# Exchanging the scratch slots of two temporaries in the mixing layers of a fused two-block network

## The chip, the cores and the metric

The kernel runs on one core of a Trainium2 chip. The metric is the device time of one execution in microseconds (us), the median of several runs. The kernel before takes 1500.32 us (three runs, 1500.16 to 1500.45).

## The reference

One call computes two blocks over a sequence of 256 tokens with 1024 features, all in float32. The first block has two attention layers (a convolution beside one attention, then two kinds of sparse attention). The second block, run after it, has two layers of this form:

```
x = x + 0.5 * swiglu(rms_norm(x, ffn1_norm[l]), ...)
h = rms_norm(x, mix_norm[l])
proj = h @ w_in[l]
y_rwkv = rwkv7_group(proj[..., :RWKV_IN], ...)     # a recurrence over time, 8 heads of 64
y_ret = retnet_group(proj[..., RWKV_IN:])          # retention, 4 heads
x = x + concat(y_rwkv, y_ret) @ w_out[l]
x = x + 0.5 * swiglu(rms_norm(x, ffn2_norm[l]), ...)
```

The recurrence updates a 64x64 state per head: S <- S*diag(w) + (S a) b^T + v k^T, y = S r. Its output is normalised per head and gated. Retention rotates q and k, masks the scores q k^T by a decay, multiplies them with v and normalises per head.

## The kernel before, in words

Features lie on the 128 partitions, the 256 tokens along the free axis. Every weight is streamed from memory once, in parts of 128x1024, through a ring: SyncE issues the load into `raw` (4 slots, line 108), ScalarE casts it to `whi` (line 115), VectorE forms the rest `wlo` (line 116); `whi` and `wlo` have 5 slots each. A projection of 256 output features takes two such parts and 48 matmuls of 256 columns (three products per weight tile: lines 129 to 131, or 306 to 308 where tokens become the output rows). Its result stands in one of two PSUM banks of the tag `mm` until VectorE or ScalarE has read it.

A mixing layer (`mix`) works on the eight heads in two units of four. Unit 0 projects k, r and v, prepares the operands (`operands`), and builds its chunk matrices (`chunks`): gram matrices (line 980), then five levels of a triangular inverse, each level a `t1` and a `dx` (line 963) on TensorE with a mask, an addition and a transpose on VectorE between them (lines 1022, 1028, 1029). Unit 1 does the same. Then `chain` runs the recurrence of both units side by side, four chunks each, and ends with the last step: mean, squares, head sums (line 900), the reciprocal root in small VectorE steps (lines 172 to 180), the head norm factors widened by ScalarE (`wide`, line 887), transposed by TensorE (`spread`, line 891), and the gate (line 1105). After that comes `retention`: the projections rq and rk (read out into `rx`, line 1149, then rotated, lines 1155 to 1160), rv in two halves, rg in two halves, then scores (line 1189, masked into `rsc`), values and norms, and the output projection.

Scratch tiles come from a pool in which a tag names a ring of slots; here `pd` and `pz` have two slots each. A new tile of a tag takes the slot of the tile two before it and may be written only when that one's readers are done, in the order in which the program asks for the tiles. In the kernel before, `pz` holds the projection read out of PSUM in `shifted` (line 852) and later the masked scores; `pd` holds the token-shifted product (line 855), `wide`, `rx` and `rgt` (the read-out gate projection of retention).

The order of the instructions on an engine is not the program's order. A list scheduler places each instruction on its engine's queue when, by its own estimate, operands and slots are free; on the chip each queue then runs in that fixed order. So a change of slots changes the order.

Of the kernel before, what the change touches and what calls it, by code (L numbers as in the profile page):

```python
# [9 lines left out]
F32 = mybir.dt.float32  # L10
# [41 lines left out]
class Net:  # L52
# [771 lines left out]
    def mix(self, tag, l, cst):  # L824
# [6 lines left out]
        with ExitStack() as c:  # L831
            psum = self.banks.using(mm=(0, 1), ch=(2, 4), ss=(3,), inv=(5, 6), y=(7, 3))
            work = c.enter_context(tc.tile_pool(name="mw", bufs=1))
# [49 lines left out]

            def spread2(rn, tag):

                wide = work.tile([128, 2, 4, 64], F32, tag="pd", name="wide", bufs=2)
                nc.scalar.copy(wide, rn[:, :, :, None].to_broadcast([128, 2, 4, 64]))
                ps = psum.tile([128, 2, S], F32, tag=tag, name="spread")
                for u in range(2):
                    for tt in range(2):  # L890
                        nc.tensor.transpose(ps[:, u, tt * 128:tt * 128 + 128],
                                            wide[:, tt, 2 * u:2 * u + 2].rearrange("p e d -> p (e d)"), ident)
                return ps
# [19 lines left out]
            def operands(q, b):  # L913
# [24 lines left out]
                for u in range(2):  # L938
                    nc.vector.scalar_tensor_tensor(kq[:, u], r[:, u], self.v(f"rk{l}", 2 * b + u), kh[:, u],
                                                   op0=OP.mult, op1=OP.mult)  # L940
                yield
                sp = spread2(rn, "inv")
                nc.vector.tensor_tensor(kk, kk, sp, op=OP.mult)
                ps = psum.tile([128, 2, S], F32, tag="inv", name="bonus")
# [90 lines left out]
            def chain(q, b):  # L1035
# [58 lines left out]
                rn = self.rsqrt(by_head(y2, "ch"), [128, 2, 4], 1.0 / 64, 64e-5, "q")  # L1094
                yield
                sp = spread2(rn, "ch")
                nc.vector.tensor_tensor(y, y, sp, op=OP.mult)
                for u in range(2):
# [42 lines left out]
    def retention(self, tag, l, psum, work, cst, units):  # L1141
        nc = self.nc
        qk = {}
        qs = {}

        def project(name):
            ps = self.proj_t(psum, (tag, name))
            q = qs[name] = work.tile([128, 2, S], F32, tag="pd", name="rx", bufs=2)
            nc.vector.tensor_tensor(q, ps, self.rsb, op=OP.mult)

        def rotate(name):
            q = qs[name]
            ps = psum.tile([128, 2, S], F32, tag="mm", name="rot")
            for u in range(2):
                nc.tensor.matmul(ps[:, u], cst["rot"], q[:, u], start=True, stop=True)
            b = lambda m: m[:, None, :].to_broadcast([128, 2, S])
            o = qk[name] = work.tile([128, 2, S], F32, tag={"rq": "pr", "rk": "pk"}[name], name=name)
            nc.vector.tensor_tensor(o, ps, b(cst["sin"]), op=OP.mult)
            nc.vector.tensor_tensor(q, q, b(cst["cos"]), op=OP.mult)
            nc.vector.tensor_tensor(o, o, q, op=OP.add)  # L1160

        project("rq")
        project("rk")
        rotate("rq")
        v = work.tile([128, 2, 512], F32, tag="op1", name="rv")
        for b in range(2):
            ps = self.proj_n(psum, (tag, "rv", b))
            if b == 0:
                rotate("rk")
            for tt in range(2):  # L1170
                nc.scalar.activation(v[:, tt, 256 * b:256 * b + 256], ps[:, tt], AF.Copy,
                                     scale=self.rstok[:, tt:tt + 1])
        g = work.tile([128, 4, S], F32, tag="op2", name="rg")
        for b in range(2):
            ps = self.proj_t(psum, (tag, "rg", b))
            t = work.tile([128, 2, S], F32, tag="pd", name="rgt", bufs=2)
            nc.vector.tensor_tensor(t, ps, self.rsh, op=OP.mult)
            self.half_silu(g[:, 2 * b:2 * b + 2], t)
        for j in range(4):
            self.ysplit(units[j // 2]["y"][:, j % 2], j)  # L1180
        op = [work.tile([128, 2, S], F32, tag=n, name="ro", bufs=2) for n in ("sw", "av")]
        o = [op[h // 2][:, h % 2] for h in range(4)]
        ps2 = psum.tile([128, 2, 4], F32, tag="ss", name="rss")

        def scores(h):
            p, j = slice(64 * (h % 2), 64 * (h % 2) + 64), h // 2
            q, k = qk["rq"][p, j], qk["rk"][p, j]
            ps = psum.tile([128, 384], F32, tag="mm", name="rs")
            nc.tensor.matmul(ps[:, 0:256], k[:, 0:128], q, start=True, stop=True)
            nc.tensor.matmul(ps[:, 256:384], k[:, 128:256], q[:, 128:256], start=True, stop=True)  # L1190
            s = work.tile([128, 384], F32, tag="pz", name="rsc", bufs=2)
            nc.vector.tensor_tensor(s[:, 0:256], ps[:, 0:256], cst["dec"][:, h], op=OP.mult)
            nc.vector.tensor_tensor(s[:, 256:384], ps[:, 256:384], cst["dec"][:, h, 0:128], op=OP.mult)
            return s

        def values(h, s):
            ps = psum.tile([128, S], F32, tag="mm", name="ro")
            w = slice(h * 128, h * 128 + 128)
            nc.tensor.matmul(ps, v[:, 0, w], s[:, 0:256], start=True, stop=False, skip_group_check=True)
            nc.tensor.matmul(ps[:, 128:256], v[:, 1, w], s[:, 256:384], start=False, stop=True, skip_group_check=True)  # L1200
            nc.scalar.copy(o[h], ps)
            oq = work.tile([128, S], F32, tag="zz", name="oq", bufs=2)
            nc.scalar.activation(oq, ps, AF.Square)
            return oq

        def norms(h, oq):
            for tt in range(2):
                nc.tensor.matmul(ps2[:, tt, h:h + 1], oq[:, tt * 128:tt * 128 + 128], self.ones[:, 0:1], start=True,
                                 stop=True)

        s = [scores(0), scores(1)]
        sq = []
        for h in range(4):
            sq.append(values(h, s[h]))
            if h < 2:
                s.append(scores(h + 2))
            if h:
                norms(h - 1, sq[h - 1])
        norms(3, sq[3])
        rn = self.rsqrt(ps2, [128, 2, 4], 1.0 / 128, 1e-6, "q")  # L1220
        for h in range(4):
            sp = self.spread(psum, lambda tt: rn[:, tt, h:h + 1].to_broadcast([128, 128]))
            nc.vector.tensor_tensor(o[h], o[h], sp, op=OP.mult)
            nc.vector.tensor_tensor(o[h], o[h], g[:, h], op=OP.mult)
            self.ysplit(o[h], 4 + h)
# [280 lines left out]
```

## Time and profile before

| what | value |
|---|---|
| median of 3 runs | 1500.32 us |
| profiled execution | 1503.37 us, of which span 1501.6 us |
| TensorE matmul busy | 1445.1 us (96%) |
| VectorE busy | 1028.8 us (69%) |
| ScalarE busy | 740.1 us (49%) |
| chain that ended last | TensorE 88%, VectorE 6%, ScalarE 4% |

The span is the time between the first and the last instruction of the profiled execution; 1.8 us lie around it. A matmul's busy time is modelled and matmuls overlap, so that 283 ns is noted for one that follows its predecessor by 0.12 us; a stretch in which TensorE counts as busy can still have room. The two mixing layers lie at about 525 to 700 us and 1110 to 1285 us.

### The profile page before, as it was taken

Reading aid. Unit: us, or ns where it says so; the run is one execution under the profiler, and the core shown is the slowest. Engines: PE = TensorE matmul, PEld = TensorE weight load, DVE = VectorE, ACT = ScalarE, POOL = GpSimd, SP = SyncE. Lnnn points to the kernel's source line nnn. Section 1 sums busy time; section 2 is a strip of 40 time slices with the busy share of each in tenths; the row PEclk is TensorE's granted clock in tenths of the full one; section 3 lists DMA queues with packets and bytes.
Section 4 is the critical chain, followed back from the end, with each engine's and each line's share of the span. In section 5 each row is a group of like instructions: output and inputs, shape, how many; then the busy total and the mean of one; then the engine's idle time right before and its main releaser. Section 6 shows DMA issues by size and latency. Waiting matters only on the chain.

```text
span 1501.6 us, 31844 instructions
## 1 busy us (share of the span) xinstructions
PE 1445.1 (96%) x13326; PEld 1381.6 (92%) x13326; DVE 1028.8 (69%) x1914; ACT 740.1 (49%) x1268; POOL 6.3 (0%) x43
## 2 busy tenths in 40 slices
PE   8899999999999999899999999999999879999997
PEld 8699979899999988789999999999998769999997
DVE  7879798976556777557755657565588655865564
ACT  6947565845444573135544445444466213554443
POOL 0000000000000000000000000000000000000000
PEclk9999999999999999999999999999999999999998
DMA  8234543365555532024555555555553103555651
GB/s 290 74 127 146 166 128 126 92 225 183 182 183 183 183 128 73 15 77 136 175 185 184 185 184 170 183 183 182 183 169 113 44 2 113 167 173 182 184 184 53
DMA packets 63600, 222.01 MB, mean 148 GB/s; under 512 B 7744, under 2 KB 9024, under 8 KB 63456
## 3 DMA queue, kind: packets, MB, share of 16 engines
q1 hardware_dynamic: 62928, 219.31, 45.9%
q8 instruction: 104, 1.70, 0.5%
q10 hardware_dynamic: 432, 0.53, 0.1%
q14 instruction: 40, 0.33, 0.1%
q0 software_dynamic: 96, 0.13, 0.0%
HBM read 218.90 MB, written 1.05 MB: 146 GB/s over the span
## 4 chain that ended last, share of the span: by engine, by line
PE 88%; DVE 6%; ACT 4%; issue 1%; DMA 1%; DVEq 0%; ACTq 0%
PE gu L129 11%; PE gu L130 11%; PE gu L131 11%; PE mm L129 6%; PE mm L130 6%; PE acc L129 6%; PE acc L131 6%; PE acc L130 6%; PE mm L131 6%; PE dx L963 1%; DVE wlo L116 1%; PE t L963 1%; PE gram L980 1%; ACT whi L115 1%; PE gu L271 1%
## 5 line engine op out<-in xcount | busy, mean ns | idle before, releaser
L115 ACT CAST whi<-raw 128x1024 fp32r<-128x1024 f32 (+1 forms) x412 | 427.1, 1040 | 459.2 <-PE gu L130 163.2
L116 DVE TENSOR_TENSOR wlo<-raw,whi 128x1024 fp32r<-128x1024 f32 (+1 forms) x412 | 499.6, 1214 | 221.4 <-ACT whi L115 221.1
L129 PE MATMUL gu<-hh,whi 128*128 128x256 f32 x1344 | 381.0, 283 | 0.1
L130 PE MATMUL gu<-hl,whi 128*128 128x256 f32 x1344 | 380.5, 283 | 0.0
L131 PE MATMUL gu<-hh,wlo 128*128 128x256 f32 x1344 | 380.3, 283 | 0.0
L129 PEld LDWEIGHTS gu<-hh,whi 128*128 128x128 f32 x1344 | 257.9, 192 | 0.6 <-issue 0.2
L130 PEld LDWEIGHTS gu<-hl,whi 128*128 128x128 f32 x1344 | 258.0, 192 | 0.0
L131 PEld LDWEIGHTS gu<-hh,wlo 128*128 128x128 f32 x1344 | 258.0, 192 | 0.0
L131 PE MATMUL acc<-mh,wlo 128*128 128x256 f32 x704 | 198.7, 283 | 0.0
L130 PE MATMUL acc<-ml,whi 128*128 128x256 f32 x704 | 198.7, 283 | 0.0
L129 PE MATMUL acc<-mh,whi 128*128 128x256 f32 x704 | 197.6, 283 | 0.2
L129 PE MATMUL mm<-hh,whi 128*128 128x256 f32 x608 | 179.2, 295 | 7.1 <-ACT whi L115 6.8
L130 PE MATMUL mm<-hl,whi 128*128 128x256 f32 x608 | 176.2, 290 | 0.0
L131 PE MATMUL mm<-hh,wlo 128*128 128x256 f32 x608 | 176.0, 289 | 0.0
L131 PEld LDWEIGHTS acc<-mh,wlo 128*128 128x128 f32 x704 | 135.2, 192 | 0.0
L130 PEld LDWEIGHTS acc<-ml,whi 128*128 128x128 f32 x704 | 135.2, 192 | 0.0
L129 PEld LDWEIGHTS acc<-mh,whi 128*128 128x128 f32 x704 | 134.2, 192 | 0.9 <-issue 0.4
L129 PEld LDWEIGHTS mm<-hh,whi 128*128 128x128 f32 x608 | 117.7, 194 | 13.1 <-ACT whi L115 6.8
L130 PEld LDWEIGHTS mm<-hl,whi 128*128 128x128 f32 x608 | 117.7, 194 | 2.4 <-issue 0.8
L131 PEld LDWEIGHTS mm<-hh,wlo 128*128 128x128 f32 x608 | 117.7, 194 | 2.0 <-issue 1.0
L246 DVE TENSOR_TENSOR t<-gu,rs 128x512 f32<-128x512 f32 x88 | 60.5, 691 | 55.0 <-PE gu L131 55.0
L137 ACT CAST mh<-g 128x256 fp32r<-128x256 f32 x88 | 35.4, 406 | 100.6 <-DVE g L249 100.6
(392 smaller groups left out, 2218.7 us busy)
## 6 DMA issues: line engine op xcount, KB each, us to landing
raw<-in_stream SPq DMA_DIRECT2D x404, 512.0 KB, 3.6
raw<-in_stream SPq DMA_DIRECT2D x4, 280.0 KB, 2.8
x<-in_x SPq DMA_DIRECT2D x4, 256.0 KB, 5.1
raw<-in_stream SPq DMA_DIRECT2D x4, 256.0 KB, 5.3
lora<-in_lora SPq DMA_DIRECT2D x2, 512.0 KB, 5.0
dec<-in_dec SPq DMA_DIRECT2D x1, 512.0 KB, 6.3
out<-o SPq DMA_DIRECT2D x2, 256.0 KB, 2.5
out<-o ACTq DMA_DIRECT2D x2, 256.0 KB, 2.5
```

Source lines behind the costliest of these rows:

```text
L115: nc.scalar.copy(hi, raw)
L116: nc.vector.tensor_tensor(lo, raw, hi.bitcast(F32), op=OP.subtract)
L129: mm(out, ah, bh, start=start, stop=False, skip_group_check=True)
L130: mm(out, ah, bl, start=False, stop=False, skip_group_check=True)
L131: mm(out, al, bh, start=False, stop=stop, skip_group_check=True)
L137: nc.scalar.copy(hi, src)
L246: nc.vector.tensor_tensor(t, ps, self.rsb, op=OP.mult)
L271: mm(ps[:, u], part, self.h[k][0], start=(i + j == 0), stop=False, skip_group_check=True)
L963: nc.tensor.matmul(ps[p, n], lhs(e, p, n), rhs(e, p, n), start=True, stop=True)
L980: nc.tensor.matmul(ps[p, n], bk[p, 4 * u + n, w], ar[p, 4 * u + n], start=True, stop=True)
```

## The change

`wide` takes its slots from `pz` instead of `pd`, and the masked scores `rsc` take theirs from `pd` instead of `pz`. Nothing is computed differently.

```
             def spread2(rn, tag):

-                wide = work.tile([128, 2, 4, 64], F32, tag="pd", name="wide", bufs=2)
+                wide = work.tile([128, 2, 4, 64], F32, tag="pz", name="wide", bufs=2)
                 nc.scalar.copy(wide, rn[:, :, :, None].to_broadcast([128, 2, 4, 64]))
...
-            s = work.tile([128, 384], F32, tag="pz", name="rsc", bufs=2)
+            s = work.tile([128, 384], F32, tag="pd", name="rsc", bufs=2)
             nc.vector.tensor_tensor(s[:, 0:256], ps[:, 0:256], cst["dec"][:, h], op=OP.mult)
```

The scheduler then orders the two mixing layers differently; both change alike, and the rest of the program hardly. Three places of the first one follow.

TensorE, the inverse of unit 1, third level, before (t1 and dx are its two products, bt a transpose of the operands, y the recurrence of unit 0):

```order
L963 MATMUL dx_7530<-t1_7456,xT_7450 64x64 x16
L1074 MATMUL y_7688<-gk_6844,vt_6890 64x64
L963 MATMUL t1_7549<-x_7449,gb_7407 64x64 x16
L1006 MATMUL bt_7567<-ident_74,bk_7397 128x128 x4
L963 MATMUL dx_7576<-t1_7456,xT_7450 64x64 x16
L963 MATMUL t1_7595<-x_7449,gb_7407 64x64 x16
```

The same level now (mm_8165 is the first half of the rv projection):

```order
L963 MATMUL t1_7549<-x_7449,gb_7407 64x64 x16
L1006 MATMUL bt_7567<-ident_74,bk_7397 128x128 x4
L307 MATMUL mm_8165<-wlo_8035,hh2_6425 128x256
L308 MATMUL mm_8165<-whi_8034,hl2_6426 128x256
L306 MATMUL mm_8165<-whi_8034,hh3_6429 128x256
L307 MATMUL mm_8165<-wlo_8035,hh3_6429 128x256
L963 MATMUL dx_7576<-t1_7456,xT_7450 64x64 x16
L308 MATMUL mm_8165<-whi_8034,hl3_6430 128x256
L306 MATMUL mm_8165<-whi_8064,hh4_6433 128x256
L307 MATMUL mm_8165<-wlo_8065,hh4_6433 128x256
```

Before, no projection stood between the levels of unit 1; now four stand ahead of this dx and eight behind it, and all of rv has moved from behind the gate to the stretch from the gram matrices to the spreads.

TensorE, the last step of the recurrence, before:

```order
L1089 MATMUL mean_7953<-uy_7687,blk64_106 128x512
L1089 MATMUL mean_7958<-uy_7689,blk64_106 128x512
L900 MATMUL sums_7963<-e2_104,t1_7956 128x2 x4
L900 MATMUL sums_7983<-e2_104,t1_7961 128x2 x4
L891 MATMUL spread_8005<-ident_74,wide_8003 128x128 x4
L891 MATMUL spread_8015<-ident_74,wide_8013 128x128 x4
L1105 MATMUL gate_8023<-wag_6669,lora_4113 128x256 x2
L1155 MATMUL rot_8157<-rx_8092,rot_4109 128x256 x2
L1105 MATMUL gate_8027<-wag_6669,lora_4113 128x256 x2
L306 MATMUL mm_8165<-whi_8034,hh0_6417 128x256
```

Its end now (mm_8299 is the first of rg's two projections):

```order
L1105 MATMUL gate_8023<-wag_6669,lora_4113 128x256 x2
L131 MATMUL mm_8299<-hh1_6421,wlo_8187 128x256
L129 MATMUL mm_8299<-hh2_6425,whi_8186 128x256
L891 MATMUL spread_8015<-ident_74,wide_8013 128x128 x4
L130 MATMUL mm_8299<-hl2_6426,whi_8186 128x256
L131 MATMUL mm_8299<-hh2_6425,wlo_8187 128x256
L129 MATMUL mm_8299<-hh3_6429,whi_8186 128x256
L130 MATMUL mm_8299<-hl3_6430,whi_8186 128x256
```

Before, rv and rg (192 matmuls) and the rotation of rk stood behind the second gate and ahead of the first scores; now 56 matmuls do. Of the others 75 stand between the gram matrices of unit 1 and the mean, and 61 between the mean and the second gate. rk's last 27 matmuls now stand between bonus and the gram matrices of unit 1, where 3 stood.

VectorE, operands of unit 0, the end of the reciprocal root (ry), before (pz_7185 is the read-out of unit 1's k, which stands 16 rows ahead of these; pz_7255 that of its r):

```order
L116 TENSOR_TENSOR wlo_7227<-raw_7224,whi_7226 128x1024
L180 SCALAR_TENSOR_TENSOR ry_6802<-rt_6803,ry_6802 128x8
L852 TENSOR_TENSOR pz_7255<-mm_7193,rs_6636 128x2x256
L116 TENSOR_TENSOR wlo_7281<-raw_7278,whi_7280 128x1024
L943 TENSOR_TENSOR kkq_6784<-kkq_6784,spread_6824 128x512
```

And now:

```order
L116 TENSOR_TENSOR wlo_7227<-raw_7224,whi_7226 128x1024
L179 SCALAR_TENSOR_TENSOR rt_6803<-rt_6803,ra_6801 128x8
L116 TENSOR_TENSOR wlo_7281<-raw_7278,whi_7280 128x1024
L180 SCALAR_TENSOR_TENSOR ry_6802<-rt_6803,ry_6802 128x8
L852 TENSOR_TENSOR pz_7185<-mm_7123,rs_6636 128x2x256
L943 TENSOR_TENSOR kkq_6784<-kkq_6784,spread_6824 128x512
```

The read-out of unit 1's k has moved behind the root, since its slot is asked for after that of `wide`; the read-out of r has moved further back, behind the first masked gram matrix, and one more cast stands ahead of the root's last step. On TensorE the spread of `wide` now stands ahead of the small products pw and pa (lines 874, 875), where before it stood behind three of their four, and 1 projection matmul instead of 12 stands between them and the first gram matrix.

## Rows read from the trace of the kernel before

**Rows 1.** The page's chart of the span in 40 slices (tenths busy; granted clock).
```profile
PE   8899999999999999899999999999999879999997
...
DVE  7879798976556777557755657565588655865564
...
PEclk9999999999999999999999999999999999999998
```

**Rows 2.** Stages of the first mixing layer; the columns' names stand first.
```profile
core 0: us, PE busy (x) PEld busy (x) DVE busy (x) ACT busy (x) POOL busy (x), PEclk, DMA share, GB/s
...
551.20:555.70 4.50, 3.21 (x13) 1.66 (x12) 4.26 (x8) 3.56 (x8) 0.00 (x0) 0.94 0.89 315
555.70:569.20 13.50, 13.50 (x132) 12.19 (x131) 11.46 (x20) 9.13 (x19) 0.21 (x2) 0.90 0.18 61
569.20:594.30 25.10, 25.00 (x451) 22.91 (x450) 16.73 (x28) 7.58 (x14) 0.00 (x0) 1.00 0.27 91
594.30:600.60 6.30, 3.21 (x24) 2.21 (x23) 4.66 (x14) 2.38 (x4) 0.00 (x0) 0.91 0.23 70
600.60:610.60 10.00, 9.38 (x124) 8.80 (x124) 6.28 (x12) 1.34 (x4) 0.00 (x0) 0.71 0.12 49
610.60:630.50 19.90, 14.94 (x415) 13.55 (x412) 10.25 (x16) 3.65 (x10) 0.00 (x0) 1.00 0.01 3
630.50:641.50 11.00, 10.56 (x296) 9.75 (x296) 4.36 (x16) 0.59 (x1) 0.00 (x0) 1.00 0.01 3
641.50:655.40 13.90, 10.34 (x45) 7.31 (x41) 9.23 (x35) 3.08 (x5) 0.00 (x0) 0.75 0.01 1
655.40:679.80 24.40, 24.34 (x197) 23.75 (x196) 14.78 (x18) 10.55 (x16) 0.00 (x0) 1.00 0.49 151
```

**Rows 3.** The last two of these stages in the second mixing layer.
```profile
1225.50:1239.30 13.80, 10.21 (x42) 7.15 (x40) 9.23 (x35) 3.08 (x5) 0.00 (x0) 0.75 0.00 1
1239.30:1263.70 24.40, 24.29 (x196) 23.77 (x196) 14.72 (x18) 10.55 (x16) 0.00 (x0) 1.00 0.42 130
```

**Rows 4.** Timeline of TensorE: start, length, idle before and releaser in brackets.
```profile
598.43 0.66 PE L891 MATMUL spread<-ident,wide 128*128 128x128 f32 x4 [1.58 <-ACT wide L887]
600.66 6.51 PE L980 MATMUL gram<-ar,bk 64*64 64x128 f32 x64 [1.57 <-DVE ar L948]
622.65 1.15 PE L963 MATMUL t<-x,gb 64*64 64x64 f32 x32 [0.89 <-DVE x L1028]
628.55 1.15 PE L963 MATMUL dx<-xT,t 64*64 64x64 f32 x32 [0.78 <-DVE t L1022]
649.18 2.04 PE L891 MATMUL spread<-ident,wide 128*128 128x128 f32 x8 [2.20 <-ACT wide L887]
653.01 1.57 PE L1155 MATMUL rot<-rx,rot 128*128 128x256 f32 x4
661.25 1.03 PE L1155 MATMUL rot<-rx,rot 128*128 128x256 f32 x4
```

**Rows 5.** The same view around the operands of unit 0.
```profile
551.19 1.13 PE L874 MATMUL pw<-wag,lora 64*128 64x256 f32 x4
553.61 0.70 PE L875 MATMUL pa<-wag,lora 64*128 64x256 f32 x2 [1.29 <-DVE pz L852]
554.23 0.66 PE L891 MATMUL spread<-ident,wide 128*128 128x128 f32 x4
```

**Rows 6.** VectorE groups of 569.2 to 594.3 us: count, busy, mean ns.
```profile
L116 DVE TENSOR_TENSOR wlo<-raw,whi 128x1024 fp32r<-128x1024 f32 x4 | 4.9, 1222 | 1.5 <-ACT whi L115 1.5
```

**Rows 7.** VectorE groups of 600.6 to 655.4 us.
```profile
L1028 DVE TENSOR_TENSOR x<-dx,x 128x512 f32<-128x512 f32 x4 | 2.8, 692 | 4.9 <-PE dx L963 4.9
L1149 DVE TENSOR_TENSOR rx<-mm,rs 128x512 f32<-128x512 f32 x2 | 1.4, 684 | 0.0
```

**Rows 8.** Timeline of VectorE, ends of the reciprocal roots of unit 0's operands and of the last step.
```profile
552.79 0.15 DVE L180 SCALAR_TENSOR_TENSOR ry<-rt,ry 128x8 f32<-128x8 f32 x1
649.23 0.17 DVE L180 SCALAR_TENSOR_TENSOR ry<-rt,ry 128x8 f32<-128x8 f32 x1
```

## The prediction, made before the changed kernel was run

> **What bounds the kernel now.** I read the page's chart first. TensorE is busy in nine tenths of nearly every slice, and the granted clock is full; what dips there are lie in the two mixing layers, where VectorE is no fuller than elsewhere [rows 1]. So the kernel is bound by TensorE except where it waits, and the stage table of the first mixing layer shows where. From 594.3 to 655.4 us, 61.1 us, memory is all but silent (50 GB/s and less after 600.6 us) and TensorE counts as busy for 3.21 + 9.38 + 14.94 + 10.56 + 10.34 = 48.4 us; VectorE has 4.66 + 6.28 + 10.25 + 4.36 + 9.23 = 34.8 us of work there [rows 2]. Neither is full: it is a chain of short steps that alternate between the two, as the timeline says (t1 waits 0.89 us for x, dx 0.78 us for the mask, the spread 2.20 us for `wide`) [rows 4]. The granted clock there falls to 0.71 and 0.75 of full in two stages [rows 2], that is, to the lower level of 1.2 GHz for part of them, after TensorE had stood idle 1.58, 1.57 and 2.20 us [rows 4]. Behind the last gate the picture flips: 655.4 to 679.8 us holds 24.34 us of TensorE work in 24.40 us at full clock [rows 2]. The second layer repeats this to 0.1 us [rows 3].
>
> So before, independent projections (rv, rg) wait behind a latency-bound chain, although their operands are there. The reason is in the slots: rq's read-out `rx` needed the slot of the last step's `wide`, and the two `mm` banks stayed full of rq and rk.
>
> **The change part by part, for one layer.**
>
> *Work taken from behind the gate.* Of the 192 matmuls in that 24.40 us stage 136 go forward. The stage is 192 steps and one rotation of 1.03 us [rows 2, 4]: (24.40 - 1.03) / 192 = 0.1217 us each. What stays is 56 x 0.1217 = 6.8 us, so 24.4 - 6.8 = **17.6 us** leave. That is the most to be had; what follows is how much of it the chain gives back.
>
> *Operands of unit 0 (551.2 to 555.7 us).* k's read-out moves behind the reciprocal root, and one cast of 1.22 us [rows 6] stands ahead of the root's last step, which ended at 552.9 us [rows 8]. The read-out is 0.68 us (as `rx`, the same shape) [rows 7], so `wide` comes 1.22 - 0.68 = 0.54 us later. What stood between root and next product (another read-out and a cast, 1.9 us) shrinks to one read-out, so nothing else is added. TensorE's own wait grows: spread now precedes pw and pa, and their 1.13 us [rows 5] no longer fill the gap. I take **+0.5**. Below, -1: less stands on VectorE ahead of the first t1 (a cast and an operand product go behind it, a read-out comes in: 1.22 + 0.69 - 0.68, nearly all of which could be gained). Above, +3.4: a longer idle gap brings the lower clock to unit 0's gram matrices as it did to unit 1's, where 0.29 x 10.0 = 2.9 us of full clock went [rows 2], on top of the 0.5.
>
> *Operands and gram matrices of unit 1 (594.3 to 610.6 us).* 24 more rk matmuls (27 against 3, 24 x 0.12 = 2.9 us) fall into the idle 1.58 + 1.57 us [rows 4], and fit. VectorE reads rk out between two products that the gram matrices need: +0.7 [rows 7]. Against this the filled gap should keep the clock, of which 2.9 us were lost. I take half of what would offset it and call the stage **0**; bounds -2.2 (all the clock) and +2.1 (three rotation steps of rq at 0.68 us between the masks, all late).
>
> *Levels of unit 1's inverse (610.6 to 630.5 us).* In: 54 projection matmuls (6.6 us), one rotation, three casts (3.7 us) and three rotation steps of rk (2.0 us) on VectorE. The nearest row is the same work in unit 0, which already had 80 such matmuls, four casts and three other read-outs: 25.1 us against 19.9 [rows 2], 5.2 us for more than is added here. Where eight matmuls (1.0 us) meet a wait of 0.89 us [rows 4] they are nearly free; the cost is the casts on VectorE, in a gap of 4.9 us over four steps [rows 7]. I scale 5.2 us by 54/80 and take off 0.5 us for the head sums of unit 0: **+3.0**, bounds 0 and +5.2.
>
> *The recurrence (630.5 to 641.5 us).* Six matmuls in all: +0.3, at most 0.7.
>
> *The last step (641.5 to 655.4 us).* Out: two read-outs `rx` (1.4 us) and the rotation of rq (1.57 us, at the lower clock) [rows 4, 7]. In: 61 matmuls (7.4 us) and three casts (3.7 us). TensorE counted 10.34 of 13.90 us at clock 0.75, so at full clock its own work is nearer 8; with 7.4 us more it is nearly full, and should run at full clock. VectorE: the second root ended at 649.4 us [rows 8]; two casts (2.4 us) and the first unit's norm (about 1.1 us) now stand ahead of that, and 3.5 us later than 649.4 is 652.9, from which widening, spread and gate end near 656.9. I take **+1.5**, bounds 0 and +4.
>
> What hides the rest: casts and loads for rv and rg come earlier, into a stretch where memory moves 1 to 49 GB/s [rows 2]; if the loads were late, a VectorE queue that waits for a cast would hold the chain, which the upper bounds of the two stages with casts include. The scores' new slots wait for rg's read-outs, which are done before rg itself can be; nothing is added.
>
> Sum for one layer: -17.6 + 0.5 + 0 + 3.0 + 0.3 + 1.5 = -12.3; I take -11.7, since casts now share 6.8 us behind the gate with the splitting of y and may cost half a microsecond there. Two layers: **-23.4 us**. The profiled execution, 1503.4 us (1501.6 of span and 1.8 around it), would become 1480.0; against the median, 3.1 us lower, 1500.3 - 23.4 = **1477 us**.
>
> **A rule that speaks against it.** Unit 0's stage of levels, with 80 matmuls among them, was 5.2 us longer than unit 1's [rows 2]. The Trainium skill, TensorE: Matmul & The Clock Gate, section "Part 2: What happens when you issue a matmul", says that matmuls stay in program order and only weight loads are pulled ahead. By that rule no step of the chain can pass a projection matmul that stands ahead of it; the trace agrees in part, since 80 matmuls are 9.7 us and only 5.2 showed.
>
> The clock's fall to 0.71 came with idle gaps of 1.6 us on either side of one spread [rows 2, 4]. The Trainium skill, same page, section "Part 1: The HAM clock gate (the "warmup" mystery)", has the slow state as the default, released by sustained activity. By it the filled gap before unit 1's gram matrices keeps the clock, and the emptier one before unit 0's loses it; the rows show the first only.
>
> **The rivals.**
> - *Nothing of the projections hides in the levels* (strict order). 54 x 0.1217 = 6.6 us instead of 3.0: the layer gains 11.7 - 3.6 = 8.1 us, 1484 us. For it: every queue is fixed. Against: the 5.2 us above. 0.12.
> - *The late read-out of k stalls unit 0*: +3.4 instead of +0.5 and the clock stays low at unit 1 too (+0.7 instead of 0): 11.7 - 3.6 = 8.1 us again, 1484 us. For it: TensorE now has nothing between 551.2 us and the spread. Against: VectorE, not TensorE, is the fuller there (4.26 of 4.50 us, 11.46 of 13.50) [rows 2]. 0.10.
> - *Everything fits and the clock stays full*: -17.6 - 1 - 2.2 + 1.5 = -19.3 for one layer, 1462 us. 0.13.
> - *Slower: filling in series.* If every matmul and cast put into the chain lengthened it, one layer would pay, from the gram matrices to the second gate, 136 matmuls (16.6 us), six casts (7.3 us) and six rotation steps (4.1 us), 28.0 us, less the 1.4 + 1.57 us that leave the last step: 25.0 against 17.6 saved, +7.4, and 1515 us. It decides once more than 70% (17.6 of 25.0) of it is in series. Against: 80 matmuls and the casts of unit 0 together cost 5.2 us. 0.05.
> - *The change doesn't do what it says*: rv still waits, for its `mm` bank, until rq's and rk's read-outs are late: 1500 us. Against: both stand ahead of unit 1's masks in the new order. 0.03.
>
> **How the numbers follow.** The forecast has 0.57 (its own range 1471 to 1483 us), the rivals 0.43 together. The range that leaves about 2 in 10 out is 1465 to 1488 us: it takes in both 1484s and most of the way to 1462. A change within 0.2% (3 us) is about what a measurement can't tell from none. Faster by more: 0.57 + 0.12 + 0.10 + 0.13 = 0.92; same 0.03; slower 0.05.
>
> **What would show it.** Right: first rs at about 668 us instead of 679.8, with 56 projection matmuls behind the second gate; rv matmuls between t1 and dx of unit 1, this stage at 22 to 23.5 us; granted clock near 1.00 in the last step. Wrong: a stage of levels above 25 us, unit 0 at clock below 0.9 up to the gram matrices, a TensorE wait for a cast among the levels, or rs as late as before.

## The result, and the profile after

The changed kernel takes 1480.72 us (median of 4 runs, 1479.06 to 1483.00); the kernel before took 1500.38 us beside it (4 runs, 1500.16 to 1502.57). The ratio is 0.9867, 95% interval 0.985 to 0.9884. Faster, as forecast; the time lies 3.7 us above the 1477 us predicted and inside the range. The profiled executions stand at 1503.37 and 1481.24 us, 22.1 us apart.

The page of the changed kernel, busy line and chart, answers to [rows 1]:

```profile
PE 1442.0 (97%) x13326; PEld 1379.1 (93%) x13326; DVE 1027.2 (69%) x1914; ACT 739.7 (50%) x1268; POOL 6.3 (0%) x43
...
PE   8899989999999989999999999999998999999997
...
DVE  7879788976565676768655558556577757865564
...
PEclk9999999999999998999999999999999999999998
```

TensorE has the same 13326 instructions in 22 us less. The dips of [rows 1] in slices 17, 32 and 33, which hold unit 1's chain of each layer, are gone. New are the 8s in slices 15 and 31 (518 to 555 and 1110 to 1147 us), which hold the operands of unit 0 of each layer, the clock's 8 in slice 16, right behind the first of them, and an 8 in slice 6, outside the mixing layers.

The stages of the first mixing layer, cut at the same events as [rows 2] (first head sums of unit 0, its first t1, first step of its recurrence, first gram matrix of unit 1, its first t1, first joint step of the recurrence, mean, end of the last gate, first rs; columns as there):

```profile
542.49:570.00 27.51, 23.26 (x171) 19.63 (x172) 21.04 (x42) 15.28 (x29) 0.31 (x3) 0.81 0.28 97
570.00:595.67 25.67, 25.37 (x458) 23.23 (x457) 18.38 (x30) 9.66 (x18) 0.00 (x0) 1.00 0.24 66
595.67:602.04 6.37, 6.37 (x50) 5.38 (x50) 4.75 (x14) 2.82 (x5) 0.00 (x0) 1.00 0.26 96
602.04:612.14 10.10, 10.10 (x150) 8.71 (x149) 9.20 (x17) 2.09 (x5) 0.00 (x0) 1.00 0.11 39
612.14:635.09 22.95, 22.95 (x459) 20.68 (x458) 14.46 (x21) 6.34 (x13) 0.00 (x0) 1.00 0.16 51
635.09:646.59 11.50, 11.50 (x304) 10.60 (x303) 4.36 (x16) 0.59 (x1) 0.00 (x0) 1.00 0.13 45
646.59:660.79 14.20, 14.20 (x103) 12.70 (x100) 10.87 (x36) 6.74 (x10) 0.00 (x0) 1.00 0.29 85
660.79:667.43 6.64, 6.64 (x57) 6.51 (x56) 5.22 (x8) 3.86 (x7) 0.00 (x0) 1.00 0.70 217
```

The first stage as it was before, in the first and in the second layer, since [rows 2] cut it otherwise:

```profile
542.99:569.23 26.24, 24.95 (x205) 21.37 (x205) 22.83 (x45) 17.85 (x33) 0.21 (x2) 0.93 0.30 102
1129.02:1153.75 24.73, 23.43 (x204) 20.19 (x205) 22.82 (x45) 17.85 (x33) 0.22 (x2) 1.00 0.31 107
```

From unit 1's operands on TensorE counts as busy all the time at full clock, where it idled 12.7 of 61.1 us before and its clock fell to 0.71 and 0.75 [rows 2]. The last stage shrinks from 24.4 to 6.64 us, and what is paid for it stands mainly in the first two stages (+1.3 and +0.6) and in the levels (+3.1). The whole stretch falls from 136.8 us (542.99 to 679.81) to 124.9 us. In the second layer it falls from 134.7 to 124.1 us; there the last two stages and the first are:

```profile
1220.08:1234.27 14.19, 14.19 (x102) 12.70 (x100) 10.86 (x36) 6.74 (x10) 0.00 (x0) 1.00 0.29 87
1234.27:1240.90 6.63, 6.63 (x57) 6.50 (x55) 5.21 (x8) 3.86 (x7) 0.00 (x0) 1.00 0.41 131
1116.80:1143.51 26.71, 22.38 (x172) 18.98 (x172) 21.04 (x42) 15.29 (x29) 0.32 (x3) 0.87 0.29 99
```

TensorE's timeline after, the places that answer to [rows 4, 5]:

```profile
554.05 1.12 PE L891 MATMUL spread<-ident,wide 128*128 128x128 f32 x4 [3.32 <-ACT wide L887]
555.09 2.08 PE L874 MATMUL pw<-wag,lora 64*128 64x256 f32 x4
558.10 0.58 PE L129 MATMUL mm<-hh,whi 128*128 128x256 f32 x1 [0.93 <-ACT sw L878]
...
602.04 1.09 PE L980 MATMUL gram<-ar,bk 64*64 64x128 f32 x16
...
655.49 0.65 PE L891 MATMUL spread<-ident,wide 128*128 128x128 f32 x4
...
667.43 0.70 PE L1189 MATMUL rs<-rq,rk 64*128 64x256 f32 x2
```

No bracket is left at unit 1's gram matrices or at the last step's spread. One has grown: unit 0's spread now waits 3.32 us, and pw, 1.13 us long before, takes 2.08 us at the lower level of the clock (0.50 from 555 to 560 us).

### The profile page after: what moved, and what is told of

Same layout as the page of the kernel before. It is cut to its first block, busy times and chain, and to the rows that moved or that the text cites. A ratio compares the mean times of both kernels' runs of the same rounds, so it can differ in the third digit from the quotient of the medians.

```text
span 1479.4 us, 31824 instructions
## 1 busy us (share of the span) xinstructions
PE 1442.0 (97%) x13326; PEld 1379.1 (93%) x13326; DVE 1027.2 (69%) x1914; ACT 739.7 (50%) x1268; POOL 6.3 (0%) x43
## 4 chain that ended last, share of the span: by engine, by line
PE 89%; DVE 4%; ACT 4%; issue 1%; DMA 1%; SPq 0%; DVEq 0%; ACTq 0%
PE gu L129 11%; PE gu L130 11%; PE gu L131 11%; PE mm L130 6%; PE mm L129 6%; PE acc L129 6%; PE acc L130 6%; PE acc L131 6%; PE mm L131 6%; PE dx L963 1%; DVE wlo L116 1%; ACT whi L115 1%; PE t L963 1%; PE gu L271 1%; PE gram L980 1%
```

## The experiments

My theory: rv and rg were held because `rx` waited for the slot of the last step's `wide`; freed, their matmuls fill TensorE's gaps in unit 1's chain. Rivals: the scores' half of the exchange matters too; it was the low clock, not the work, that cost the time; the price in the levels is VectorE's casts, as the prediction had it. The kernel before read 1500.4 to 1502.8 us in the batches, so each ratio is against its own batch.

**Which half of the exchange.** One edit of the two at a time:

```
e1   wide  tag "pd" -> "pz"      rsc stays in "pz"
e2   wide  stays in "pd"         rsc  tag "pz" -> "pd"
```

> Only `wide` goes to the tag pz; the masked scores `rsc` stay there too. Theory (what frees rv and rg is that rx no longer waits for the slot of the last step's wide): the whole gain, 1478 to 1483 us, first rs near 667 us in the first mixing layer, 56 projection matmuls behind its last gate. Rival (both halves of the exchange are needed, since scores and wide now meet in one tag): the scores of head 0 wait for the read of wide, rs to norm spread grows by 1 us or more and the gain halves, 1488 to 1492 us.

> Only the masked scores go to the tag pd; `wide` stays there as before. Theory: nothing of the gain, 1498 to 1503 us, rs near 679 us, 192 projection matmuls behind the last gate. Rival (part of the gain comes from the scores' shorter queue behind rg): 1490 us or less.

Measured: `wide` alone 1479.26 us (1478.77 to 1479.87), ratio 0.9842 (0.9826 to 0.9858); the scores alone 1505.38 us (1502.95 to 1506.53), ratio 1.0009 (0.9998 to 1.002), above the 1498 to 1503 us that I expected, beside a kernel before that itself read 1502.8 us in this batch. The stage from the last gate's start to rs, first in the kernel with `wide` alone, then with the scores alone:

```profile
657.68:665.35 7.67, 7.67 (x63) 7.43 (x61) 6.25 (x10) 3.86 (x7) 0.00 (x0) 1.00 0.64 207
```
```profile
654.08:679.46 25.38, 25.32 (x202) 24.32 (x200) 15.72 (x20) 10.55 (x16) 0.00 (x0) 1.00 0.48 144
```

The whole gain is in `wide`'s slot. The scores' half brings nothing: ten projection matmuls (52 instead of 42) move ahead of the spread of retention's norms, which then comes 15.2 instead of 13.8 us after rs.

**The slot, or who shares it.** Leave `wide` in `pd` and take `rx` away from it, into two slots that are free by then:

```
-  q = qs[name] = work.tile([128, 2, S], F32, tag="pd", name="rx", bufs=2)
+  q = qs[name] = work.tile([128, 2, S], F32, tag={"rq": "kh", "rk": "e1"}[name], name="rx")
```

> The kernel before, with one edit: `rx` of rq and rk takes the single slots of kh and e1, which the operands of unit 1 leave free; `wide` and the scores stay where they were. Theory (the wait of rx behind wide is the cause, not where wide lies): the same advance, 56 projections behind the last gate, and unit 0 as before, 1476 to 1480 us. Rival (the gain comes from wide lying in another tag): 1497 to 1503 us. Against the theory would also be a rotation that now waits for kh's last reader, with rs near 675 us.

Measured: 1483.86 us (1482.17 to 1485.77), ratio 0.9873 (0.9855 to 0.9891); rs at 668.22 us with 56 projections behind the gate. So the sharing of `rx` and `wide` is the cause, wherever it is broken. My number was 4 to 8 us too low, and this kernel's timeline of TensorE says why:

```profile
595.75 1.02 PE L1155 MATMUL rot<-rx,rot 128*128 128x256 f32 x4
599.02 1.12 PE L891 MATMUL spread<-ident,wide 128*128 128x128 f32 x4 [2.25 <-ACT wide L887]
601.71 1.54 PE L980 MATMUL gram<-ar,bk 64*64 64x128 f32 x12 [1.57 <-DVE ar L948]
```

The rotation of rq now stands ahead of unit 1's spread, whose wait grows from 1.58 [rows 4] to 2.25 us while the gap before the gram matrices stays. First recurrence step to gram matrices: 8.38 us, against 6.37 in the changed kernel.

**Unit 0's loss.** Choose the slot of `wide` by its place; in the second kernel the scores stay in `pz` as well:

```
-  wide = work.tile([128, 2, 4, 64], F32, tag="pz", name="wide", bufs=2)
+  wide = work.tile([128, 2, 4, 64], F32, tag={"inv": "pd", "ch": "pz"}[tag], name="wide", bufs=2)
```

("inv" is passed by the operands, "ch" by the recurrence.)

> On the changed kernel, only the recurrence's `wide` is in pz; the operands' `wide` goes back to pd. Theory (unit 0 lost 1.3 and 0.6 us per layer, and its clock, because k's read-out pz had to wait for the operands' wide): the granted clock from 555 to 565 us is back near 0.9, the stages of unit 0 are back at 26.2 and 25.1 us, and, with 39 instead of 56 projections behind the last gate, 2 to 3 us per layer come off: 1474 to 1478 us. Rival (unit 0's loss is only the order of pw and pa, or the casts that come earlier from elsewhere): 1480 to 1482 us, the clock there still near 0.5.

> As the kernel in which only the recurrence's wide is in pz and the operands' wide in pd, with the masked scores back in pz. Theory (the scores' half of the exchange does nothing, and unit 0 keeps the order of before): 1476 to 1478.5 us, the fastest of all, rs to norm spread 13.8 instead of 15.2 us with ten matmuls fewer in it. Rival (scores and wide in one tag now meet, since the recurrence's wide is the last reader before them): rs to norm spread above 15 us, 1480 us or more.

Measured: 1477.86 us (1477.15 to 1478.17), ratio 0.9832 (0.9816 to 0.9848), and 1476.94 us (1475.60 to 1477.49), ratio 0.983 (0.9817 to 0.9842). The windows of the second kernel: unit 0's first two stages, then all from its first recurrence step to rs.

```profile
541.38:567.62 26.24, 24.95 (x204) 21.36 (x204) 22.83 (x45) 17.82 (x33) 0.21 (x2) 0.93 0.31 102
567.62:592.67 25.05, 24.96 (x449) 22.88 (x449) 16.68 (x28) 7.56 (x14) 0.00 (x0) 1.00 0.30 90
...
592.67:664.59 71.92, 69.48 (x1088) 61.85 (x1088) 47.81 (x109) 21.47 (x40) 0.00 (x0) 1.00 0.20 66
```

The same stretch in the changed kernel:

```profile
595.67:667.43 71.76, 71.76 (x1113) 64.58 (x1112) 48.84 (x109) 22.43 (x40) 0.00 (x0) 1.00 0.23 74
```

Unit 0 is back at the times of before, so its loss came from the slot of the operands' `wide`. What that slot moves comes back all together, k's read-out, the cast ahead of the root, pw and pa, so the run doesn't say which of them cost the time; that it was k's read-out is not shown. But from there to rs this kernel needs as long as the changed kernel with 25 matmuls fewer: in the first of the two kernels unit 1's spread, its `wide` in `pd`, waits 1.58 us again, and a projection behind it 0.83 us for `rx`.

**A kernel that beats both.** Only unit 0's operands go back to `pd`; unit 1's and the recurrence's `wide` take `pz`, and the scores stay in `pz`:

```
-  def spread2(rn, tag):
+  def spread2(rn, tag, at="pz"):
...
-  sp = spread2(rn, "inv")
+  sp = spread2(rn, "inv", ("pd", "pz")[b])
```

> On the changed kernel, `wide` of unit 0's operands alone goes back to pd (of unit 1's operands and of the recurrence it is in pz), and the scores back to pz. Theory (TensorE-bound from unit 1's operands to rs; what can still be had are idle gaps): unit 0 as in the kernel before (24.7 or 26.2 us, then 25.05), and 12 + 21 projections of rv stand around the spread of unit 1's operands, where TensorE waited 1.6 us; 21 instead of 39 are left behind the last gate; 1472 to 1476 us. Rival (the chain of unit 1 is late instead, since VectorE reads rq and rk ahead of it): operands and gram matrices of unit 1 grow from 17 us to 20 us and more, and the time is 1477 to 1481 us.

Measured: 1473.36 us (1472.68 to 1477.22), ratio 0.9809 (0.9793 to 0.9826), the lowest median of all; three of its four runs lie below every run of the two kernels above, though its interval overlaps theirs. The stretch from unit 0's first recurrence step to rs, in both layers:

```profile
594.05:663.64 69.59, 69.28 (x1084) 62.58 (x1084) 45.06 (x104) 21.02 (x38) 0.00 (x0) 0.98 0.20 62
1166.64:1234.97 68.33, 68.02 (x1084) 61.16 (x1083) 44.92 (x104) 21.03 (x38) 0.00 (x0) 1.00 0.20 64
```

With 1084 instead of 1113 rows it is 2.2 and 3.4 us shorter than in the changed kernel: 29 matmuls at 0.1217 us are 3.5 us, and the first layer lost some clock in the last step (0.98 over the stretch). That is no gain by itself, since 25 of these matmuls lie in unit 0's first stage again; the gain is that this stage, with 106 instead of 81 projection matmuls, takes no longer. Unit 0 is as before in the first layer (26.20 and 25.05 us); in the second its first stage took 27.77 us at a clock of 0.88. Where 33 projection matmuls now stand around unit 1's spread, no wait is left there. My rival had a part of it: first recurrence step to t1 is 17.3 us instead of 16.5, but not the 20 us at which it would have decided.

**The clock by itself.** The kernel before with matmuls that nobody reads, put behind mean, sums and spread, 24 in each layer and 12 in the second kernel (`range(2)`):

```
+  def filler():
+      fl = psum.tile([128, 2, S], F32, tag="inv", name="fill")
+      for u in range(4):
+          nc.tensor.matmul(fl[:, u % 2], rot, cos, start=True, stop=True)
```

> The kernel before, with 20 matmuls of 128x128 by 128x256 in each layer's last step (mean, sums, spread) whose result nobody reads; every projection stays where it was. Theory (the gain is work that leaves the end of the layer, not the clock): rs stays within 2 us of 679.8, the granted clock of the last step rises from 0.74 to 0.95 or more, and the time is 1497 to 1504 us; what the full clock gives back to the chain's own matmuls is at most about 1 us per layer. Rival (it was mainly the lower clock that the change took away): 1490 us or less, although nothing moved.

> The kernel before with 10 to 12 matmuls of 128x128 by 128x256 whose result nobody reads, half as many as in the filler run; about half of them stand in the last step, the rest fall into unit 1's levels. Theory (the clock alone is worth little): the granted clock of the last step 0.85 to 1.00, the step 11 to 13 us instead of 13.1, rs at 678 to 681 us, and 1497 to 1505 us. Rival (the filler run was slower only because its matmuls stood in series, and the full clock alone is worth 5 us per layer): rs at 675 us or less and 1491 us or less.

Measured: 1509.66 us (1506.93 to 1513.67), ratio 1.0054 (1.0038 to 1.007), and 1506.99 us (1504.66 to 1507.47), ratio 1.0027 (1.0018 to 1.0035). Both missed my range, upwards. In the kernel with fewer of them, the last step (mean to the last gate's start) and the stage from there to rs:

```profile
642.18:653.13 10.95, 9.87 (x54) 7.21 (x50) 7.35 (x32) 3.08 (x5) 0.00 (x0) 1.00 0.01 1
653.13:679.54 26.41, 25.49 (x201) 24.44 (x201) 16.64 (x22) 10.54 (x16) 0.00 (x0) 1.00 0.47 140
```

At full clock the last step, with 7 of the 12 fillers in it, takes 10.95 instead of 12.89 us (cut the same way), 1.9 us less. Yet rs comes at 679.5 us: the 1.1 us longer recurrence, where part of the fillers fell, and the stage behind the gate, 1.0 us longer, take it back; of that 1.0 us, 0.86 are a wait for rk's read-out `rx` ahead of the first projection. In the second layer the levels also took 21.62 us at a granted clock of 0.92. So the clock's part in the last step is real, about 2 us for each layer. The fillers did not touch the other stage at a low clock, unit 1's gram matrices, which stayed at 0.72 in the first layer; from that clock and the 9.99 us of this stage before, I estimate that the full clock can be worth at most 0.28 x 9.99 = 2.8 us there; no run isolates it. Together that is less than half of the 11 us: the rest is work that left the end of the layer, while here the 192 projections stayed behind the gate.

**The price in the levels: casts or matmuls.** Take VectorE's casts away, and then add matmuls:

```
e6   lo = hi if key[1] in ("rv", "rg") else <the tile of before>   # and no subtraction for these
e7   for _ in range(13 if tt == 0 and k == 0 else 1):              # in the projection of rv
         mm(ps[:, tt, :n], hh[:, q], hi, start=(tt == 0 and k == 0), ...)
```

> The changed kernel without VectorE's casts of the low parts of the rv and rg weights; their products take the high part in its place, so that the matmuls are as many as before and four casts of 1.22 us per half of each weight leave VectorE. Left out: the low parts of these two weights. Theory (from the gram matrices to rs TensorE is full, and the levels' 3.1 us are its matmuls): 1478 to 1482 us, although VectorE has some 10 us less to do in each layer. Rival (the 3.1 us are the casts, as the prediction had it): 1472 to 1476 us. Here 89 instead of 56 projections stand behind the last gate.

> The changed kernel, with the first product of each half of rv done 13 times over (24 more matmuls in each layer, 2.9 us at 0.1217 us). Theory (the chain's gaps are used up, TensorE is full from the gram matrices to rs): they cost their whole time, +5 to +6.5 us, 1485.5 to 1487.5 us. Rival (there is still idle time beside the chain, as there was before the change, when 136 matmuls cost only a third of their time): +2 us or less, 1481 to 1483 us.

Without the casts: 1481.27 us (1481.15 to 1481.35), ratio 0.986 (0.9847 to 0.9873), no gain, although VectorE's busy time from the head sums to the norms' spread fell by 8.5 us in each layer. The order changed with it: ten projection matmuls fewer stand in the levels of unit 1, which took 1.22 us less, 0.12 us for each:

```profile
609.26:630.99 21.73, 21.65 (x457) 19.65 (x457) 11.49 (x18) 5.32 (x13) 0.00 (x0) 1.00 0.11 40
```

With more matmuls: 1490.19 us (1489.93 to 1490.35), ratio 0.9919 (0.9906 to 0.9932). From unit 1's gram matrices to rs, first the changed kernel, then the one with more matmuls in both layers:

```profile
602.04:667.43 65.39, 65.39 (x1064) 59.20 (x1063) 44.10 (x96) 19.61 (x36) 0.00 (x0) 1.00 0.23 72
```
```profile
604.07:672.33 68.26, 68.26 (x1088) 62.03 (x1087) 44.47 (x96) 19.72 (x36) 0.00 (x0) 1.00 0.22 70
1180.53:1248.81 68.28, 68.28 (x1088) 62.04 (x1087) 44.48 (x96) 19.71 (x36) 0.00 (x0) 1.00 0.19 63
```

24 matmuls more, 2.87 us longer: 0.120 us each, their whole time. (The total rose by more, 9.5 us, because an attention layer of the first block uses the same helper: my expectation missed that. By the first mixing layer's head sums it was 2.9 us later.) So there is no room left beside the chain in this stretch, and VectorE isn't its bound.

## Why the prediction was right, step by step

- *Work from behind the gate*, -17.6 predicted: 24.37 to 6.64 us, -17.7. The 56 matmuls left cost the 6.8 us foreseen, so the half microsecond I set aside for casts beside them wasn't needed.
- *Operands of unit 0*, +0.5: **mis-sized**. It was +1.3 in the first layer and +2.0 in the second, and another +0.6 in the levels behind, for which I had no term. `wide` came 0.42 us later (I had 0.54), but I took the upper bound, the lower clock, for the less likely case. It came in both layers: spread waits 3.32 and 3.40 us with nothing before it, and the clock is 0.50 from 555 to 560 us, 0.87 over the stage of the second layer. So one of my signs of being wrong came true: up to unit 0's first gram matrix, from 542.49 to 558.61 us, the clock was 0.81, against 0.89 before. The rival on k's late read-out had the direction, at +3.4 too much; its other half, a low clock at unit 1 too, did not come.
- *Operands and gram matrices of unit 1*, 0: 6.38 to 6.37 and 9.99 to 10.10 us, with the projections that fill the gaps and the clock at 1.00.
- *Levels of unit 1*, +3.0: 19.84 to 22.95, +3.1. The size was right, **the reason was wrong**: I put it down to casts on VectorE. The run without them gained nothing. What does give the size is TensorE's own work: before, it was idle for 19.9 - 14.94 = 5.0 us of this stage [rows 2], and 54 projection matmuls and a rotation, 7.6 us, overfill that by 2.6. The row I scaled from, unit 0's levels, was full already (25.00 of 25.10 us), so scaling it gave the right size by luck. The timelines show how it comes about, first TensorE's (rows between left out), then VectorE's, after and before:

```profile
619.60 0.39 PE L308 MATMUL mm<-whi,hl 128*128 128x256 f32 x1
619.82 0.28 PE L306 MATMUL mm<-whi,hh 128*128 128x256 f32 x1
...
620.54 0.28 PE L306 MATMUL mm<-whi,hh 128*128 128x256 f32 x1
620.75 1.15 PE L963 MATMUL t<-x,gb 64*64 64x64 f32 x32
...
628.98 0.28 PE L308 MATMUL mm<-whi,hl 128*128 128x256 f32 x1
629.10 1.03 PE L1155 MATMUL rot<-rx,rot 128*128 128x256 f32 x4
630.06 1.15 PE L963 MATMUL t<-x,gb 64*64 64x64 f32 x32
```
```profile
619.72 0.69 DVE L1028 TENSOR_TENSOR x<-dx,x 128x512 f32<-128x512 f32 x1 [1.45 <-PE dx L963]
```
```profile
621.81 0.69 DVE L1028 TENSOR_TENSOR x<-dx,x 128x512 f32<-128x512 f32 x1 [1.25 <-PE dx L963]
```

  x is ready at 620.41 us, but t1 starts at 620.75, 0.34 us later, behind eight projection matmuls; before it started 0.15 us after x (622.50 and 622.65 [rows 4]). From t1 to t1 the first three levels take 4.24 to 4.37 us instead of 3.97 to 4.05. The fourth, with the rotation (1.03 us) in it, takes 4.95, and the last, with 21 projection matmuls, 5.03 us; before they took 3.97 and 3.87 us, so that these two pay 2.1 of the 3.1 us. The Trainium skill, TensorE: Matmul & The Clock Gate, "Part 2: What happens when you issue a matmul", has matmuls in program order; these rows agree. That doesn't make the rival of strict order right: 54 projection matmuls and a rotation, 7.6 us, cost 3.1.
- *The recurrence*, +0.3: 11.04 to 11.50. *The last step*, +1.5: **mis-sized**, 13.92 to 14.20, +0.3. I put the end of the second root 3.5 us later and had widening, spread and gate take 4.0 us from there. Counted from the mean the root ended 3.0 us later (10.9 instead of 7.9 us), and the rest took 3.3 us, where before, with a rotation between and most of it at the lower clock, it took 6.0 ([rows 8] for the root before; after):

```profile
657.31 0.16 DVE L180 SCALAR_TENSOR_TENSOR ry<-rt,ry 128x8 f32<-128x8 f32 x1
```

- *Sum*, -11.7 for a layer: -11.9 and -10.6. The two misses, in unit 0 and in the last step, nearly cancel, so that the sum is nearer than its parts by luck. The second layer gains less because its unit 0 had been at full clock before (24.73 us); that it repeats the first to 0.1 us held only for the two stages in [rows 3].
- *From profile to median.* -23.4 predicted, -22.1 between the profiled executions: 1.3 of the 3.7 us. The rest is that I let the profiled execution stand 3.1 us over the median on both sides; the changed kernel's stands 0.5 over. Up to half of those 3.1 us can be the low clock in unit 0 of the first layer (26.24 against 24.73 us).
- *Rivals.* "Filling in series" would have made the chain 25.0 us longer in a layer; from unit 0's first recurrence step to the last gate it grew by 4.0 us (the stage rows, 3.1 of it in the levels). Only what comes on top now is in series, as the added matmuls show. "Everything fits" failed in unit 0 and in the levels.

The Trainium skill, the same page, "Part 1: The HAM clock gate (the "warmup" mystery)", has the slow state as the default, released by sustained activity. Of the two things that I drew from it, the rows after show both: full clock through the filled gap before unit 1's gram matrices, and 0.50 behind the emptied one of unit 0. The last section has rows that the rule alone doesn't tell.

## What to carry to other kernels

Where independent work waits behind a latency-bound chain although its operands are there, look for the scratch slot that two temporaries share, and move only the one that blocks, by place and not by name: the same move that freed rv delayed unit 0, and giving unit 0 its slot back was worth another 5 to 6 us (1479.26 to 1473.36 us, measured in two batches; by the ratios 0.9842 and 0.9809). Price filler in a chain by where it falls: free until the gaps are used up, at its full time after that, and at a fraction of a microsecond wherever it stands in the queue ahead of a step that is already ready. A gap that a move empties can cost the clock for the next microseconds, as it did in unit 0.

## What the runs showed of the hardware that was not expected

The same instructions with the same idle time kept the clock in one layer and lost it in the other. In the kernel before, pa waits 1.29 us in both layers ([rows 5] for the first); after it, one microsecond in each layer, and the wait in the second:

```profile
556.00:557.00 1.00, 1.00 (x6) 1.00 (x6) 1.00 (x3) 1.00 (x4) 0.11 (x1) 0.50 0.95 270
1142.00:1143.00 1.00, 1.00 (x10) 0.96 (x9) 1.00 (x3) 1.00 (x4) 0.11 (x1) 1.00 1.04 414
```
```profile
1139.63 0.70 PE L875 MATMUL pa<-wag,lora 64*128 64x256 f32 x2 [1.29 <-DVE pz L852]
```

Over the eight profiled kernels with that order, the first stage took 24.7 us 5 times, 26.2 to 26.3 us 10 times and 27.8 us once; over the four with the order of the changed kernel 26.6 to 27.7 us each time. What decides it in a given layer stays open.

Nor does it take an idle gap. In the kernel with `wide` chosen by unit, TensorE counted as busy from 640 to 657 us of the first layer, projection matmuls behind the head sums, and the clock fell all the same; in the second layer the same instructions kept it, and the last step took 11.16 instead of 12.42 us:

```profile
640.00:653.00 13.00, 13.00 (x250) 11.25 (x250) 6.21 (x19) 3.48 (x5) 0.00 (x0) 1.00 0.13 43
654.00:657.00 3.00, 3.00 (x17) 3.00 (x16) 2.60 (x15) 1.91 (x3) 0.00 (x0) 0.50 0.00 0
```

In the kernel with the scores alone moved, the recurrence of the second layer, 11.04 us at full clock in the first, took 12.42 at 0.82:

```profile
1215.98:1228.40 12.42, 11.91 (x297) 11.23 (x297) 4.37 (x16) 0.58 (x1) 0.00 (x0) 0.82 0.02 4
```
